# Gate weights scattered into DRAM tables, and two wide passes over the second expert matrix in the first layer

## The chip, the cores and the metric

The kernel runs on one core of one Trainium2 chip. The metric is the device time of one execution in microseconds (us); lower is better. "First layer" is `l = 0` in the code and "second layer" is `l = 1`.

## What is computed

Two layers of a backbone over 512 latent tokens (tiles 0 to 3, 128 tokens each) and 256 context tokens (tiles 4 and 5). The second layer only has to produce the latent tiles. Each layer is token mixing (projection, three kinds of heads, output projection), then the expert retrieval that the change is about:

```python
def peer(h, wq, subkeys, u, v):
    q = (h @ wq).reshape(t, 8, 2, 128)
    s = einsum('thpd,hpnd->thpn', q, subkeys)            # 8 heads, 2 halves, 128 keys each
    s_top, i_top = top_k(s, 16)
    cand = s_top[:, :, 0, :, None] + s_top[:, :, 1, None, :]
    best, pos = top_k(cand, 16)                          # 16 of 128*128 experts per head
    gate = softmax(best)
    a = gelu(einsum('cd,chkd->chk', h, u[expert]))
    return einsum('chk,chkd->cd', gate * a, v[expert])
```

A token thus has 8 x 16 = 128 picks among 16384 experts of 1024 numbers each.

## The kernel before

`peer` (L945) does each layer's retrieval in stages. **Routing and picking** (`routing`, `picks`, `pick`) finds each token's 128 experts and gates. **Two up passes** (`upass`, L994, halves 0 and 1) stream the first expert matrix, 128 slices of 512 KB, and compute every expert's activation for three "dense" tiles (`self.dense`): a slice is split into two half-precision parts (high by ScalarE; low by VectorE or GpSimd, L1003 to L1006), 24 products of 128x384 follow, and Gelu. Two tiles' activations stay in SBUF (tiles `P`), the third's go to DRAM (`spill`). For the tiles that are not dense, `gather` (L912) fetches each pick's row with 128 indirect DMAs on the GpSimd queue (L924), with a dot product on VectorE (L930) each.

**The weight of every expert for every token** must then be laid out as a matrix, expert by token. `Scatter.step` (L1157) builds it: for eight tokens at a time VectorE makes one-hot matrices (L1176, `oi` and `oj`), multiplies one by the gates (L1180, `og`), TensorE multiplies the two (L1185, L1186), and the product is copied or multiplied into `P` (L1190 to L1196).

**Passes over the second expert matrix** (`vpass`, L1032): one for each pair of tiles in `self.groups`, three in the first layer and two in the second. A pass streams 128 slices of 512 KB, splits each (high L1048 on ScalarE; low L1050 on VectorE or L1052 on GpSimd, by `VDVE`), and adds 12 products of 128x512 a slice into four PSUM banks (L1065). `Scatter.at` splits the dense tiles' weights two slices at a time (L1126).

The order of the work is set in two steps. `tick` lets each background generator (`rg` routing, `bg` gathers) advance by a rate for each slice (`RATES`, `RRATE`, L1026, L1029, L1069), and a scheduling layer then fixes each engine's instruction order by priority and data dependency. Each engine runs its list strictly in that order, and so does the SP queue, which issues nearly all plain DMAs. The zeroing of the change goes into `project` (L357), the loop over 12 column chunks with three tile pairs each.

Of the kernel before, what the change touches and what calls it, by code (L numbers as in the profile page):

```python
# [25 lines left out]
US = 64.0  # L26
PS = 16.0
NEG = -1e30
TB = 8
# [3 lines left out]
RATES = {0: (2.0, 1.4, 0.8, 0.9, 0.9, 0.9, 0.0, 0.0), 1: (1.2, 1.3, 0.6, 0.6, 0.0, 0.0)}  # L33
RRATE = (0.9, 0.85)
# [6 lines left out]
WADA = 7  # L41
RL1, RL2 = 1, 0
PF = (1, 1)
UP1 = (24, 24)
SC0 = (12, 12)
PRATE = (0.5, 0.5)
VDVE = ((1, 3), (1, 3), (3,))


class Hybrid:  # L50
    def __init__(self, tc, aps, out):
        self.tc, self.nc, self.i, self.out = tc, tc.nc, aps, out
        self.dbg = {}
        self.bg = []
        self.rg = []
        self.lo_ins = None
# [15 lines left out]
    def consts(self):  # L72
# [12 lines left out]
        nc.vector.tensor_copy(self.iox, io)  # L85
        self.mhalf = c.tile([128, 8], F32, name="mhalf")
# [150 lines left out]
    def layer(self, l, last):  # L237
        with ExitStack() as es:
            self.l, self.last = l, last
            self.rt, self.h2T, self.h2d = {}, {}, {}  # L240
            self.groups = ((2, 3), (0, 1)) if last else ((2, 3), (4, 5), (0, 1))
            self.dense = (2, 3, self.groups[1][1])
            self.picked = [t for g in self.groups for t in g if t not in self.dense]
            tiles = XTILES if last else XTILES + CTILES
            self.mid = {t: self.tc.dram_tile([128, D], F32, name=f"mid{l}_{t}") for t in tiles}
# [20 lines left out]
    def mixers(self, l, last, wes):  # L266
# [11 lines left out]
        with ExitStack() as e:  # L278
            nap = self.pool(e, "nqkv")
            self.naT = nap.tile([128, 4, 2, T], F16, name="naT")  # L280
            self.nav = [nap.tile([128, 2, 2, 256], F16, name=f"nav{p}") for p in range(3)]
            hp = self.pool(e, "hT", 3)
# [14 lines left out]
            self.flush(self.rg)  # L297
            self.flush(self.bg)
# [58 lines left out]
    def project(self, l, last, hp, pool, ps, ap_, att_es, xs):  # L357
# [29 lines left out]
        for ch in range(12):  # L387
# [5 lines left out]
            for pr in (1, 0, 2):  # L393
# [9 lines left out]
                self.tick(self.rg, 1)  # L403
                self.tick(self.bg, RATE_NA if ch < 6 else RATE_DF)
# [280 lines left out]
    def wout(self, l, es, last):  # L685
# [3 lines left out]
        self.h2U = [self.lp.tile([128, KC, 384], F16, name=f"h2U{x}") for x in "hl"]  # L689
# [121 lines left out]
    def picks(self, l, tiles, sv, si, pool):  # L811
        for t in tiles:
            yield from self.pick(l, t, sv[t], si[t], pool)
            if t in self.picked:
                self.bg.append(self.gather(l, t))

# [21 lines left out]
    def pick(self, l, t, sv, si, pool):  # L838
# [25 lines left out]
        st = self.lp.tile([128, 2, 16, 8], F16, name="st", bufs=4 if self.last else 6)  # L864
        sg = self.lp.tile([128, 16, 8], F32, name="sgate", bufs=4 if self.last else 6)
# [27 lines left out]
        nc.vector.tensor_tensor(sg, sg, sm[:, None, :].to_broadcast([128, 16, 8]), op=OP.mult)  # L893
        ix = None
        if t in self.picked:
            ix = self.lp.tile([128, 16, 8], I32, name="ix", bufs=3)
            ef = pool.tile([128, 16, 8], F32, name="ef")
            nc.vector.tensor_scalar(ef, st[:, 0], 128.0, float(l * 16384), op0=OP.mult, op1=OP.add)
            nc.vector.tensor_tensor(ix, ef, st[:, 1], op=OP.add)
            ix = ix.rearrange("p k h -> p (k h)")  # L900
        self.rt[t] = (st.rearrange("p a k h -> p a (k h)"), sg.rearrange("p k h -> p (k h)"), ix)
# [10 lines left out]
    def gather(self, l, t):  # L912
        nc = self.nc
        _, sg, ix = self.rt[t]
# [4 lines left out]
        a = self.lp.tile([128, 128], F32, name="a", bufs=1)  # L919
        rows = []  # L920
        for k in range(128 + AHEAD):
            if k < 128:
# [3 lines left out]
                    in_offset=bass.IndirectOffsetOnAxis(ap=ix[:, k:k + 1], axis=0)))  # L926
                rows.append(r)
            if k >= AHEAD:
                r = rows[k - AHEAD]
                nc.vector.scalar_tensor_tensor(r, r, 1.0, hp, op0=OP.mult, op1=OP.mult,  # L930
                                               accum_out=a[:, k - AHEAD:k - AHEAD + 1])
            if k < 127 + AHEAD:
                yield
        nc.scalar.activation(a, a, AF.Gelu)
        nc.vector.tensor_tensor(sg, a, sg, op=OP.mult)
        self.done.add(t)
        yield
# [3 lines left out]
    def need(self, t):  # L941
        while t not in self.done:
            self.step(self.bg, 1)

    def peer(self, es, l, last, h2s):  # L945
        nc = self.nc
        self.done = set()
        self.hpp = self.pool(es, "hp", 1, space=PSUM)
        self.pw = self.pool(es, "pw", 2, space=PSUM)
        self.gp = self.pool(es, "gat", 3)  # L950
        self.spill = self.tc.dram_tile([128, 128, 128], F32, name=f"spill{l}")
        self.big = [[self.pool(es, "bigA")], []]
        sc = Scatter(self, (2, 3), True)
        sc.P[0] = [self.table(0, 0)]
        rk = ExitStack()
        with ExitStack() as e:
# [4 lines left out]
            groups = ((0, 1), (2, 3)) if last else ((4, 5), (2, 3, 0, 1))  # L961
            self.unscored = len(groups)
            self.rg += [self.routing(l, rt, ps, t, rp) for t in groups]
            self.upass(l, 0, sc, self.pw, "pw", RATES[l][0], RRATE[l])
# [4 lines left out]
        sc.P[1] = [self.table(1, 0)]  # L969

        def more():
# [3 lines left out]
            sc.P[1].append(self.table(1, 1))  # L975

        with ExitStack() as e:
            ps = self.pool(e, "ups", 4, space=PSUM)
            self.upass(l, 1, sc, ps, "pa", RATES[l][1], PRATE[l], more)
        self.accp = self.pool(es, "acc", 1, space=PSUM)  # L980
        for n, tiles in enumerate(self.groups):
            if n == 2:
# [3 lines left out]
            follow = Scatter(self, self.groups[n + 1]) if n + 1 < len(self.groups) else None  # L986
            self.vpass(l, tiles, int(tiles[0] > 3), sc, follow, RATES[l][2 + 2 * n:4 + 2 * n])
            sc = follow
# [5 lines left out]
    def upass(self, l, half, sc, ps, tag, rate, rrate, more=None):  # L994
        nc = self.nc
        ahead = [sc.step(0)] if half else []
        ut = self.i["ut"][l]
        hh, hl = self.h2U
        def load(jj):
# [10 lines left out]
        for jj in range(64):  # L1010
# [6 lines left out]
            for k in range(KC):  # L1017
                self.mm3(pa[:, :384], uh[:, 0, k], uh[:, 1, k], hh[:, k], hl[:, k], k == 0, k == KC - 1)
# [250 lines left out]
```

## Time and profile before

| | |
|---|---|
| median of 3 runs | 4867.58 us (4862.76 to 4879.73) |
| the profiled execution's own time | 4873.35 us |
| its span, first to last instruction | 4871.5 us |
| busy share of the span | PE 84%, PEld 49%, DVE 75%, ACT 45%, POOL 47% |
| mean granted TensorE clock | 0.930 of full speed |

PE is TensorE's matmul, PEld its weight load, DVE is VectorE, ACT is ScalarE, POOL is GpSimd. The span has the following stages. First layer: mixing and output projection to 620.7 us, up passes to 1477.5, passes over the second matrix to 2873.0. Second layer: mixing to 3317.9, up passes to 4073.9, passes over the second matrix to 4853.8. The shares above are means over these stages; what bounds one stage is read from a table by stage.

### The profile page before, as it was taken

Reading aid. Unit: us, or ns where it says so; the run is one execution under the profiler, and the core shown is the slowest. Engines: PE = TensorE matmul, PEld = TensorE weight load, DVE = VectorE, ACT = ScalarE, POOL = GpSimd, SP = SyncE. Lnnn points to the kernel's source line nnn. Section 1 sums busy time; section 2 is a strip of 40 time slices with the busy share of each in tenths; the row PEclk is TensorE's granted clock in tenths of the full one; section 3 lists DMA queues with packets and bytes.
Section 4 is the critical chain, followed back from the end, with each engine's and each line's share of the span. In section 5 each row is a group of like instructions: output and inputs, shape, how many; then the busy total and the mean of one; then the engine's idle time right before and its main releaser. Section 6 shows DMA issues by size and latency. Waiting matters only on the chain. (4 is left out here: it accounts for less than half of the span.)

```text
span 4871.5 us, 79464 instructions
## 1 busy us (share of the span) xinstructions
PE 4102.9 (84%) x30416; PEld 2392.5 (49%) x30416; DVE 3665.2 (75%) x6812; ACT 2188.7 (45%) x3704; POOL 2269.5 (47%) x1557
## 2 busy tenths in 40 slices
PE   4987888977887887787788989878887899997998
PEld 3665465743553333333334447746564554443443
DVE  7677648898779999898899443565767689998663
ACT  4556344444443343333333455655444444454443
POOL 3223223456666666555533432233246665563443
PEclk8997899998999988999999999979999999999999
DMA  5421345657877777887768653124566776555665
GB/s 173 143 86 37 123 141 169 216 190 239 282 260 250 257 252 252 278 275 265 281 212 287 219 184 94 40 85 136 163 200 206 260 272 206 166 183 176 200 205 176
DMA packets 379869, 955.11 MB, mean 196 GB/s; under 512 B 43632, under 2 KB 158800, under 8 KB 379488
## 3 DMA queue, kind: packets, MB, share of 16 engines
q1 hardware_dynamic: 296000, 675.74, 42.5%
q0 software_dynamic: 73888, 268.53, 15.6%
q10 hardware_dynamic: 9600, 5.77, 0.4%
q8 instruction: 238, 3.90, 0.3%
q14 instruction: 143, 1.17, 0.1%
HBM read 920.49 MB, written 29.41 MB: 195 GB/s over the span
## 5 line engine op out<-in xcount | busy, mean ns | idle before, releaser
L1052 POOL TENSOR_TENSOR hl<-s,hl 128x1024 f16<-128x1024 f32 x384 | 880.1, 2296 | 873.8 <-ACT hl L1048 856.6
L1065 PE MATMUL acc<-hl,gst 128*128 128x512 f16 x3456 | 827.1, 388 | 4.9 <-ACT gst L139 4.9
L930 DVE SCALAR_TENSOR_TENSOR r<-r,hp 128x1024 f32<-128x1024 f32 x512 | 618.7, 1212 | 279.6 <-DMA r<-peer_u,ix 278.7
L924 POOL DMA_INDIRECT r<-peer_u,ix x512 | 572.1, 1117 | 428.7 <-DVE r L930 219.3
L1048 ACT ACTIVATE hl<-s 128x1024 f16<-128x1024 f32 x480 | 503.5, 1055 | 581.7 <-PE acc L1065 280.7
L1065 PEld LDWEIGHTS <-gst 128*128 128x128 f16 x4608 | 452.5, 100 | 607.4 <-issue 116.0
L1065 PE MATMUL acc<-hl,P 128*128 128x512 f16 x2304 | 564.6, 389 | 57.6 <-POOL hl L1052 30.2
L1065 PEld LDWEIGHTS <-P 128*128 128x128 f16 x3072 | 296.3, 99 | 428.7 <-issue 95.0
L166 PE MATMUL pw<-h2Uh,hl 128*128 128x384 f16 x1024 | 353.6, 345 | 56.2 <-ACT gst L1022 56.1
L168 PE MATMUL pa<-h2Uh,hl 128*128 128x384 f16 x1024 | 345.8, 338 | 63.6 <-POOL hl L153 36.6
L153 POOL TENSOR_TENSOR hl<-s,hl 128x1024 f16<-128x1024 f32 x136 | 299.0, 2200 | 170.1 <-ACT hl L152 85.1
L1185 PE MATMUL pw<-og,oi 128*128 128x64 f16 x2560 | 203.8, 197 | 205.7 <-DVE og L1180 199.1
L168 PE MATMUL pw<-h2Uh,hl 128*128 128x384 f16 x1024 | 352.5, 344 | 23.5 <-DVE hl L143 17.7
L167 PE MATMUL pw<-h2Ul,hl 128*128 128x384 f16 x1024 | 352.8, 345 | 0.0
L1050 DVE TENSOR_TENSOR h2Ul<-h2Uh,h2Ul 128x1024 f16<-128x1024 f32 x160 | 259.4, 1621 | 123.7 <-ACT h2Ul L1048 123.7
L166 PE MATMUL pa<-h2Uh,hl 128*128 128x384 f16 x1024 | 345.3, 337 | 1.6 <-ACT hl L152 1.6
L167 PE MATMUL pa<-h2Ul,hl 128*128 128x384 f16 x1024 | 345.2, 337 | 0.0
L1176 DVE TENSOR_TENSOR oi<-iox,sT 128x1024 f16<-128x1024 f16 x320 | 321.9, 1006 | 27.5 <-PE pw L1186 26.3
L1065 PE MATMUL acc<-h2Ul,gst 128*128 128x512 f16 x1152 | 289.6, 395 | 53.9 <-DVE h2Ul L1050 53.9
L168 PEld LDWEIGHTS <-hl 128*128 128x128 f16 x2048 | 208.3, 102 | 251.9 <-POOL hl L153 53.8
L151 ACT ACTIVATE s<-s 128x1024 f32<-128x1024 f32 x136 | 143.7, 1057 | 417.7 <-DMA s<-ut 392.7
L1180 DVE TENSOR_TENSOR og<-oj,gT 128x1024 f16<-128x1024 f16 x320 | 322.5, 1008 | 0.6
(297 smaller groups left out, 9587.7 us busy)
## 6 DMA issues: line engine op xcount, KB each, us to landing
s<-peer_v SPq DMA_DIRECT2D x480, 512.0 KB, 4.3
s<-ut SPq DMA_DIRECT2D x256, 512.0 KB, 4.2
h2Uh<-peer_v SPq DMA_DIRECT2D x160, 512.0 KB, 4.0
wq<-peer_wq SPq DMA_DIRECT2D x128, 256.0 KB, 3.8
wst<-w_in SPq DMA_DIRECT2D x96, 256.0 KB, 3.1
r<-w_ada SPq DMA_DIRECT2D x48, 512.0 KB, 5.3
h2T<-w_ada SPq DMA_DIRECT2D x32, 512.0 KB, 3.6
spill<-gst SPq DMA_DIRECT2D x64, 256.0 KB, 4.6
```

What stands on the lines that cost most here:

```text
L153: self.lo_ins = nc.gpsimd.tensor_tensor(lo, w, hi, op=OP.subtract)
L166: nc.tensor.matmul(out, ah, bh, start=start, stop=False)
L167: nc.tensor.matmul(out, ah, bl, start=False, stop=False)
L168: nc.tensor.matmul(out, al, bh, start=False, stop=stop)
L924: self.queue_behind(nc.gpsimd.indirect_dma_start(out=r, out_offset=None, in_=self.i["peer_u"], in_offset=bass.IndirectOffsetOnAxis(ap=ix[: ...
L930: nc.vector.scalar_tensor_tensor(r, r, 1.0, hp, op0=OP.mult, op1=OP.mult, accum_out=a[:, k - AHEAD:k - AHEAD + 1])
L1048: nc.scalar.activation(vh[:, 0], v, AF.Copy)
L1050: nc.vector.tensor_tensor(vh[:, 1], v, vh[:, 0], op=OP.subtract)
L1052: self.lo_ins = nc.gpsimd.tensor_tensor(vh[:, 1], v, vh[:, 0], op=OP.subtract)
L1065: nc.tensor.matmul(acc[s][hf], w, vh[:, x, hf * 512:hf * 512 + 512], start=j == 0 and i == 0, stop=j == 127 and i == 2)
L1176: nc.vector.tensor_tensor(out.rearrange("p t (i x) -> p t i x", x=2), io.rearrange("p (i x) -> p i x", x=2)[:, None].to_broadcast([128, TB ...
L1180: nc.vector.tensor_tensor(og.rearrange("p z t (j x) -> p (z t) j x", x=2), oj.rearrange("p t j -> p (t j)")[:, None].to_broadcast([128, 2, ...
```

## The change

- **Tables.** `Scatter` is gone. Each tile has a `Table` of 8 MB in DRAM, [128 x 128 experts, 128 tokens]. It is filled with zeros during the token mixing by eight DMAs of 1 MB (`clear`, on SP). Then each of a token's 128 picks is written as one 4-byte element at its place by indirect DMAs on the GpSimd queue (`put`): one DMA writes one pick of each of the 128 tokens, 128 DMAs fill a tile, and each group of 16 (a head) waits until the group before it has landed. `vpass` reads the table back two slices at a time (`get`, 128 KB) and multiplies by the activations (`weigh`).
- **Equal picks.** Two heads of a token may pick the same expert; later writes would hide earlier ones. `pick` thus computes for each pick the sum of the gates of all equal picks: 128 VectorE instructions of 128x128 for each tile (`gjk`).
- **Four dense tiles in the first layer** (2, 3, 4, 5; products of 128x512 in the up passes, two tiles spilled), so only tiles 0 and 1 are gathered there (before: 4, 0 and 1). In the second layer 2, 3 and 1 are dense and 0 is gathered, as before.
- **Two passes instead of three** over the second matrix in the first layer, with three tiles each: (2, 3, 4) and (5, 0, 1). The second layer keeps two passes of two tiles.
- **All low splits in `vpass` on VectorE** (`VDVE`).
- Before each pass `need` issues everything that is missing in its tiles' tables. New rates `SRATES` (puts for each slice) and changed `RATES`, `RRATE`.

```diff
-RATES = {0: (2.0, 1.4, 0.8, 0.9, 0.9, 0.9, 0.0, 0.0), 1: (1.2, 1.3, 0.6, 0.6, 0.0, 0.0)}
-RRATE = (0.9, 0.85)
+RATES = {0: (1.6, 1.5, 1.3, 1.3, 0.0, 0.0), 1: (1.2, 1.2, 0.9, 0.9, 0.0, 0.0)}
+SRATES = {0: (2.5, 4.0, 2.5, 4.0, 4.0, 4.0), 1: (2.5, 3.0, 1.5, 2.5, 4.0, 4.0)}
+RRATE = (1.2, 1.0)
...
-VDVE = ((1, 3), (1, 3), (3,))
+VDVE = (0, 1, 2, 3)
...
-            self.groups = ((2, 3), (0, 1)) if last else ((2, 3), (4, 5), (0, 1))
-            self.dense = (2, 3, self.groups[1][1])
+            self.groups = ((2, 3), (1, 0)) if last else ((2, 3, 4), (5, 0, 1))
+            self.dense = (2, 3, 1) if last else (2, 3, 4, 5)
...
+                self.tick(self.zg, 2)
...
+        for k in range(128):
+            jk = pool.tile([128, 128], BF16, name="gjk")
+            nc.vector.scalar_tensor_tensor(jk, e, e[:, k:k + 1], g, op0=OP.is_equal, op1=OP.mult,
+                                           accum_out=o[:, k:k + 1])
...
+    def need(self, tiles):
+        while not all(self.tables[t].full for t in tiles):
+            self.step(self.rg, 1)
             self.step(self.bg, 1)
+            self.step(self.sq, 4)
...
+    def weigh(self, tiles, j, g, u):
...
+        if tiles[0] == self.dense[0]:
+            nc.vector.tensor_tensor(g[:, 0:2], g[:, 0:2], self.col(j // 64, j % 64, 2), op=OP.mult)
+        for s, x in u.items():
+            nc.vector.tensor_tensor(g[:, s], g[:, s], x, op=OP.mult)
+        pr = self.sp.tile([128, 2, len(tiles), 2, 128], F16, name="gst", bufs=GST)
+        self.split(pr[:, 0], pr[:, 1], g)
+        return pr
...
+    def clear(self):
+        o = self.o
+        for c in range(0, 128 * 128, ZC):
+            self.before.append(o.nc.sync.dma_start(self.view()[:, c:c + ZC].rearrange("i (r n) -> i r n", r=4),
+                                                  o.zero[:, None].to_broadcast([128, 4, ZC // 4])))
+            yield
+
+    def put(self, h, to, values, c, step):
...
+        for k in range(16):
+            ins = o.nc.gpsimd.indirect_dma_start(
+                out=self.d, out_offset=bass.IndirectOffsetOnAxis(ap=to[:, k, h:h + 1], axis=0),
+                in_=values[:, c + step * k:c + step * k + 1], in_offset=None)
...
+            self.behind(ins, self.before)
+            o.queue_behind(ins)
+            now.append(ins)
+            if k == 15:
+                self.before = now
...
+    def get(self, dst, j):
+        ins = self.o.nc.sync.dma_start(dst, self.view()[:, j * 128:j * 128 + 256].rearrange("p (j t) -> p j t", t=128))
+        self.behind(ins, self.before)
```

**The order on GpSimd at the end of the first layer's up passes.** `hl` is the low split of a slice of the first matrix, `r<-peer_u` a gather, `table_4` the table of tile 4. Before:

```order
L153 TENSOR_TENSOR hl<-s_16661,hl 128x1024
L924 DMA r<-peer_u,ix 128x1024 x3
L153 TENSOR_TENSOR hl<-s_16760,hl 128x1024
L924 DMA r<-peer_u,ix 128x1024 x2
L153 TENSOR_TENSOR hl<-s_16824,hl 128x1024
L924 DMA r<-peer_u,ix 128x1024 x4
L1052 TENSOR_TENSOR hl<-s_16988,hl 128x1024
```

After:

```order
L1184 DMA table_4_104<-gs,to 2097152x1 x4
L157 TENSOR_TENSOR hl<-s_18101,hl 128x1024
L947 DMA r<-peer_u,ix 128x1024
L1184 DMA table_4_104<-gs,to 2097152x1 x4
L157 TENSOR_TENSOR hl<-s_18144,hl 128x1024
L947 DMA r<-peer_u,ix 128x1024 x2
L1184 DMA table_4_104<-gs,to 2097152x1 x4
L947 DMA r<-peer_u,ix 128x1024
L1184 DMA table_4_104<-gs,to 2097152x1 x4
```

`s_18144` is the last slice of the up passes that GpSimd splits. From there to the last put of table 4 stand 112 puts and 30 gathers; the pass over (2, 3, 4) reads that table.

**The same engine at the end of the second layer's up passes**, where the table of tile 3 is the last that the pass over (2, 3) reads. After:

```order
L157 TENSOR_TENSOR hl<-s_41028,hl 128x1024
L947 DMA r<-peer_u,ix 128x1024 x2
L1184 DMA table_2_26534<-gs,to 2097152x1 x3
L947 DMA r<-peer_u,ix 128x1024
L1184 DMA table_2_26534<-gs,to 2097152x1 x3
L947 DMA r<-peer_u,ix 128x1024 x2
L1184 DMA table_2_26534<-gs,to 2097152x1 x7
L947 DMA r<-peer_u,ix 128x1024
L1184 DMA table_2_26534<-gs,to 2097152x1 x4
L947 DMA r<-peer_u,ix 128x1024
L1184 DMA table_2_26534<-gs,to 2097152x1 x5
L1184 DMA table_3_26535<-gs,to 2097152x1 x16
```

Here `s_41028` is the last slice that GpSimd splits. Behind the last row shown, 4 puts of table 0 and 16 of table 3 (one head) alternate until table 3 is full. From the last split to there stand 178 puts and 7 gathers. Before, no put existed and a pass's own split followed the gathers at once.

## Rows read from the trace of the kernel before

**Rows 1.** Busy time by stage (from:to, length, engines, clock, DMA), nine stages of both layers.

```profile
core 0: us, PE busy (x) PEld busy (x) DVE busy (x) ACT busy (x) POOL busy (x), PEclk, DMA share, GB/s
620.70:1114.30 493.60, 427.06 (x4131) 303.42 (x4129) 380.70 (x1463) 216.16 (x430) 204.67 (x174) 0.94 0.56 180
1114.30:1477.50 363.20, 292.56 (x2071) 172.60 (x2069) 290.05 (x476) 148.36 (x256) 229.40 (x159) 0.92 0.79 266
1477.50:1987.90 510.40, 398.88 (x2584) 188.26 (x2585) 498.38 (x623) 187.64 (x234) 329.59 (x199) 0.91 0.71 250
1987.90:2491.30 503.40, 396.90 (x2582) 186.43 (x2582) 453.36 (x663) 192.03 (x296) 260.84 (x169) 0.93 0.77 268
2491.30:2873.00 381.70, 355.26 (x2002) 164.31 (x2002) 241.33 (x348) 150.42 (x196) 144.06 (x66) 0.99 0.72 239
3317.90:3760.50 442.60, 375.70 (x3266) 254.26 (x3265) 297.27 (x1077) 210.50 (x431) 185.48 (x156) 0.93 0.55 177
3760.50:4073.90 313.40, 276.52 (x2071) 167.07 (x2069) 229.82 (x317) 144.26 (x250) 201.08 (x133) 0.97 0.76 263
4073.90:4493.90 420.00, 377.18 (x2606) 184.86 (x2607) 396.25 (x425) 189.14 (x239) 225.50 (x96) 0.96 0.54 174
4493.90:4853.80 359.90, 349.26 (x1996) 164.00 (x1993) 194.79 (x275) 166.25 (x245) 152.31 (x64) 0.99 0.63 201
```

**Rows 2.** The same view for line 1065 alone (PE, PEld): a gap, and a half pass.

```profile
2474.40:2491.20 16.80, 0.00 (x0) 0.13 (x1) 0.64 0.73 250
2701.40:2873.00 171.60, 167.93 (x768) 75.28 (x768) 0.99 0.64 203
```

**Rows 3.** Costliest groups: line, engine, operation, tile, count | busy us, mean ns | idle before.

```profile
L1180 DVE TENSOR_TENSOR og<-oj,gT 128x1024 f16<-128x1024 f16 x320 | 322.5, 1008 | 0.6
```

**Rows 4.** The same view: VectorE's splits and the multiply into `P`.

```profile
L1050 DVE TENSOR_TENSOR h2Ul<-h2Uh,h2Ul 128x1024 f16<-128x1024 f32 x160 | 259.4, 1621 | 123.7 <-ACT h2Ul L1048 123.7
L141 DVE TENSOR_TENSOR pl<-w,ph 128x768 f16<-128x768 f32 x64 | 60.9, 951 | 39.2 <-ACT ph L139 39.1
L1191 DVE TENSOR_TENSOR P<-pw,P 128x256 f32<-128x256 f32 x128 | 47.7, 413 | 4.7 <-PE pw L1186 4.6
```

**Rows 5.** The gathers on GpSimd: duration ns min/median/max, landing, and the page's group (mean).

```profile
L924 POOL DMA_INDIRECT r<-peer_u,ix x512: 932/962/1957, 804.8 to 4054.7; - x171
...
DMA to landing us min/median/max: 4.1/5.8/8.8
...
L924 POOL DMA_INDIRECT r<-peer_u,ix x512 | 572.1, 1117 | 428.7 <-DVE r L930 219.3
```

**Rows 6.** GpSimd's other work: small plain DMAs that it issues, and low splits.

```profile
L95 POOL DMA_DIRECT2D g1col<-g1col x2: 564/572/580, 2.2 to 3.2; - x2
...
L153 POOL TENSOR_TENSOR hl<-s,hl 128x1024 f16<-128x1024 f32 x136 | 299.0, 2200 | 170.1 <-ACT hl L152 85.1
```

**Rows 7.** Plain DMAs: KB each, median us from issue to landing.

```profile
gsp<-spill SPq DMA_DIRECT2D x128, 128.0 KB, 3.2
```

**Rows 8.** VectorE's dot products over 32 elements (line 624) and 1024 (line 930).

```profile
L624 DVE SCALAR_TENSOR_TENSOR lamj<-lp x6: 179/182/192, 73.7 to 2719.2; 128x32 f32<-128x32 f32 x6
L624 DVE DVE_READ_ACCUMULATOR lamj<-lp x6: 77/80/82, 73.8 to 2719.3; 128x1 f32 x6
...
L930 DVE SCALAR_TENSOR_TENSOR r<-r,hp 128x1024 f32<-128x1024 f32 x512 | 618.7, 1212 | 279.6 <-DMA r<-peer_u,ix 278.7
```

**Rows 9.** Columns of Rows 1: the last 18 slices of both layers' first up pass.

```profile
988.00:1114.30 126.30, 96.24 (x582) 55.44 (x580) 118.33 (x437) 56.16 (x88) 66.51 (x42) 0.89 0.57 186
3640.00:3760.50 120.50, 96.14 (x655) 58.54 (x653) 97.24 (x322) 56.89 (x95) 71.76 (x48) 0.93 0.58 193
```

**Rows 10.** Columns of Rows 1: the projection of the first layer.

```profile
66.60:296.00 229.40, 202.80 (x1879) 154.47 (x1879) 157.38 (x296) 127.22 (x225) 54.12 (x39) 0.95 0.44 136
296.00:413.60 117.60, 103.01 (x979) 82.55 (x977) 76.01 (x145) 69.15 (x155) 26.07 (x21) 0.94 0.14 40
```

More of the change, by code (lines that the diff above doesn't have):

```diff
@@ L688, in wout @@
         ps = self.pool(es, "wps", 2, space=PSUM, side="right")
-        self.h2U = [self.lp.tile([128, KC, 384], F16, name=f"h2U{x}") for x in "hl"]
+        self.h2U = [self.lp.tile([128, KC, 128 * len(self.dense)], F16, name=f"h2U{x}") for x in "hl"]
         a4, b3, xs = {}, {}, {}
@@ L815, in picks @@
                 self.bg.append(self.gather(l, t))
+            else:
+                self.sq += [self.tables[t].put(h, self.rt[t][2], self.rt[t][0], h, 8) for h in range(8)]
     def top16(self, v, ix, src, rest):
@@ L968, in peer @@
         self.big[1].append(self.pool(es, "bigB0", side="right"))
[L969 removed]
+        self.P[1] = [self.table(1, 0)]
         def more():
@@ L974, in more @@
             self.big[1].append(self.pool(es, "bigB1", side="right"))
-            sc.P[1].append(self.table(1, 1))
+            self.P[1].append(self.table(1, 1))
         with ExitStack() as e:
             ps = self.pool(e, "ups", 4, space=PSUM)
-            self.upass(l, 1, sc, ps, "pa", RATES[l][1], PRATE[l], more)
+            self.upass(l, 1, ps, "pa", PRATE[l], more)
+        pws.close()
         self.accp = self.pool(es, "acc", 1, space=PSUM)
         for n, tiles in enumerate(self.groups):
-            if n == 2:
+            self.need(tiles)
+            if n == 1 and not last:
                 r = lambda: self.gp.tile([128, D], F32, name="r")
@@ L992, in table, with col, upass @@
         return self.big[half][c].tile([128, 2, 32 if half else 64, 128], F32, name="P")
-    def upass(self, l, half, sc, ps, tag, rate, rrate, more=None):
+    def col(self, half, jj, n=1):
+        w = 32 if half else 64
+        p = self.P[half][jj // w]
+        return p[:, :, jj % w:jj % w + n] if n > 1 else p[:, :, jj % w]
+    def upass(self, l, half, ps, tag, rrate, more=None):
         nc = self.nc
-        ahead = [sc.step(0)] if half else []
         ut = self.i["ut"][l]
         hh, hl = self.h2U
+        nd = len(self.dense)
+        sb = 4 // (nd - 2)
         def load(jj):
@@ new lines, in upass, with weights @@
+            self.tick(self.bg, RATES[l][half])
+            self.tick(self.sq, SRATES[l][half])
+    def weights(self, tiles, j):
+        nc = self.nc
+        n = len(tiles)
+        g = self.sp.tile([128, n, 2, 128], F32, name="gt", bufs=2)
+        u = {}
+        for s, t in enumerate(tiles):
+            self.tables[t].get(g[:, s], j)
+            if t in self.spill:
+                u[s] = self.sp.tile([128, 2, 128], F32, name="gsp")
+                nc.sync.dma_start(u[s], self.spill[t][:, j:j + 2])
+        return g, u
```

292 lines of the change are left out of this document (116 added, 176 removed).

## The prediction

> **What bounds the kernel now.** I read the busy time by stage first, since the shares of the whole span (PE 84%, DVE 75%, POOL 47%) mix stages with different limits. In the first layer's first two passes over the second matrix DVE is busy 498 of 510 us and 453 of 503; where no weights are built any more, in the third, it is 241 of 382 and PE 355 [rows 1]. What fills DVE there is `Scatter.step`: one of its three large operations alone, `og`, takes 322.5 us [rows 3]. The second layer is the same in small: 420 us for the pass beside the scatter, 360 for the one after it. PE's own speed shows in the second half of the third pass: 768 products of 128x512 in 171.6 us, so .2234 us each, at a granted clock of .99, 2.4 GHz [rows 2].
>
> POOL, which has idle time everywhere, matters for what follows: in the second up passes it is busy 229 of 363 us and 201 of 313 [rows 1], with low splits and gathers.
>
> **The passes.** Removed: all of `Scatter.step`. Added for each pair of slices: a table read, one multiply by the activations, a split. If PE sets the pace, the first layer's two passes take 2 x 2304 x .2234 = 1029 us and one gap of 16.8 [rows 2], 1046 against 1395.5; the second layer's take 2 x 1536 x .2234 = 686 and 17, 703 against 779.9. That is -349 and -77. DVE covers it: for each slice one low split of 1.26 to 1.62 us, half of a 128x768 split of .95, and half of three multiplies of .41 [rows 4], some 2.7 us against PE's 4.0 (18 products). The first pass's early slices also carry 65 gathers and their dot products, for which I add 25: **-400**. Bounds: -426, and -330 if DVE sets the pace in half a pass.
>
> **What POOL must now issue before the first pass.** A put is an indirect DMA of 128 elements; none is in the trace. The nearest row is the gather, also one indirect DMA with 128 indices: .962 us median on POOL, 1.117 in the mean [rows 5]. Below it lies a small plain DMA issued from POOL, .56 [rows 6]. I take .962, because the 128 addresses are there to be worked out in both, and gather means for gathers.
>
> First layer. The first up pass multiplies 128 columns more: 1536 products x a quarter of .2234 = 86 us on PE, 493.6 to 580. In the second, the order shows on POOL 50 low splits, 106 gathers and 249 puts: 50 x 2.2 [rows 6] + 106 x 1.117 + 249 x .962 = 468 us, at 95% busy 493, where PE needs 64 slices x 24 x .2234 = 343 and the pass took 363. Each split stands between puts, so POOL sets the pace. Behind the last split stand 112 puts and 30 gathers until table 4 is full: 108 + 33 = 141 us, in which PE has no work, since `need` stands ahead of the pass. Landing (5.8 [rows 5]), a table read (3.2 [rows 7]) and one multiply and split add 11, and PE's last two slices hide about as much. Sum 580 + 493 + 141 = 1214 against 856.8: **+357**. The remaining tables 5, 0 and 1 (319 puts and 82 gathers, 398 us) lie beside the first pass of 515 us and cost nothing there; at 1.3 us a put that cover would be gone.
>
> Second layer. The first up pass keeps its three dense tiles and its 442.6. The second has 50 splits, 81 gathers and 188 puts: 110 + 90 + 181 = 381, at 95% 401. Behind the last split stand 178 puts and 7 gathers: 171 + 8, and, since a head waits for the head before it to land, 8 x (5.8 - 4 x .962) = 16: 195. Sum 442.6 + 401 + 195 = 1039 against 756.0: **+283**.
>
> That makes 727 puts on the path (361 and 366). The trace shows POOL at work for the whole of a gather. The Trainium skill would have it otherwise: in "DMA: Bandwidth & Descriptors", section "Anatomy of one DMA — SWDGE (gpsimd) path", dispatch is about 50 ns and descriptor generation is small, "You can emit a lot of descriptors before the incremental cost shows up". By it a put would cost POOL an estimated .1 us, the second up passes would keep their length, 45 and 69 us of waits would stand ahead of the passes, and the time would be an estimated 4770. The .962 us of the gathers speaks against that.
>
> **The sums of equal picks on DVE.** 128 instructions of 128x128 a tile with an accumulated output. The nearest rows: .182 us for 32 elements and .08 for reading the accumulator; 1024 elements take 1.21, so 1.04 ns an element [rows 8]. That gives .28 + .08 = .36 us, 46 us a tile, in ten uninterrupted blocks. In the first layer six blocks (276 us) come before the first pass's start. DVE idles 8 us in the last 18 slices of the first up pass and 105 before them [rows 1, 9]; the 86 us of wider products are more room: 199 in all, 77 short. Those are not just late: a gather on POOL waits for the dot product that frees its buffer, and low splits stand behind it. Some of it lies beside the second up pass: I take +60. In the second layer four blocks, 184 us, stand against 145 idle [rows 1, 9]: +25. Together **+85**, between 0 (all beside POOL's queue) and 460 (none hidden).
>
> **Zeros.** 48 MB in the first layer's projection on SP's queue among the `w_in` loads. There the DMAs move 136 GB/s at a share of .44, then 40 [rows 10]; elsewhere 250 at .71 [rows 1], about 350 when full. 48 MB in 229 us are 220 GB/s more: 356, just full. I add 9 us, and 7 for the 32 MB of the second layer: **+15**, between 0 and 60 (a few loads late).
>
> **Sum:** -400 + 357 + 283 + 85 + 15 = +340. The profiled execution took 4873, so 5213; it is 6 above the median of the runs shown, so about 5207: I say **5205**.
>
> **Rivals.**
> 1. *Puts are cheap (the other side).* POOL only starts a put, and the DMA engines do the rest. With p the price of a put, the sum is 340 - 733 x (.962 - p): 765 us for each us on 727 puts at 95% busy, less 32 for the heads' waits. It turns at p = .50 us. At .40 the second layer's second up pass is back at PE's pace (313 instead of 290), and the time is 4867 + 340 - 412 + 23 = **4820**. For: an element of 4 bytes moves almost nothing. Against: even the plain DMAs of [rows 6] take .56, and the gather's time is issue, not transfer. Chance .10. The section of the Trainium skill named above is the rule behind this one.
> 2. *The landing sets the pace.* The program gives each put one of eight completion semaphores, so eight are under way at most; if 4-byte writes land after 12 us instead of 5.8, a put costs 1.5 and the sum grows by 733 x .538 = 394: **5600**. For: 128 separate writes. Against: gathers with 128 rows of 4 KB land in 8.8 at most [rows 5]. Chance .05.
> 3. *The sums of equal picks are not hidden at all*: 460 instead of 85, **5580**. For: 94% busy DVE in the last 18 slices [rows 9]. Against: the last three blocks of the first layer stand behind the splits that PE waits for. Chance .05.
> 4. Everything nearly cancels, with puts about .5: 4868. Chance .03.
>
> **How the numbers follow.** The forecast, POOL's issue of puts as the bound, has .77 and a range of its own from 5000 to 5450 (puts from .75 to 1.12, the sums of picks from 0 to 250). Rival 1, 2 and 3 lie mostly outside; the range reaches down to half of the way to rival 1: 4850 to 5450, which leaves out .20. Within .3% (15 us) counts as no change; slower by more than that are the forecast and rivals 2 and 3, .87; the same .03; faster .10.
>
> **What would show it.** Right: puts of about .96 us on POOL; POOL busy nearly throughout the second up passes, which take some 490 and 400 us; PE idle for some 140 us ahead of the first layer's first pass, waiting for a table, and 195 in the second; half passes without a gather at .223 us a product; blocks of 46 us on DVE; the projection longer by some 10 us. Wrong: a put below half a microsecond, up passes at their old length, or passes that run slower than PE, with DVE or the table reads as what ended its waits.

## The result and the profile after

The changed kernel takes **5755.84 us** (median of 4 runs, 5751.85 to 5765.23) against 4871.85 for the kernel before beside it: ratio 1.1818, interval 1.1791 to 1.1845. It is slower, as forecast, but by 884 us and not by 340; the time lies above the predicted range. Two of the versions below, half the indices and the memset on VectorE, also had executions 2% and 4% longer than the profiled one (5938, and three between 5890 and 5913), and only the profiled one is compared.

Busy time by stage of the changed kernel, columns as in [rows 1]: the projection, then for the first layer the two up passes, the wait ahead of the first pass, and the passes in three pieces; for the second layer the two up passes, the wait, and the passes.

```profile
66.90:409.80 342.90, 303.37 (x2827) 236.26 (x2826) 228.05 (x425) 193.62 (x373) 80.48 (x58) 0.95 0.73 248
621.00:1244.00 623.00, 504.96 (x4131) 299.88 (x4130) 508.50 (x2307) 223.73 (x432) 272.04 (x238) 0.92 0.45 140
1244.00:1857.70 613.70, 404.32 (x1537) 160.51 (x1534) 335.41 (x1038) 156.48 (x255) 479.10 (x413) 0.83 0.51 164
1857.70:2034.20 176.50, 0.00 (x0) 0.00 (x0) 38.76 (x63) 3.96 (x8) 133.25 (x137) 0.51 0.35 103
2034.20:2376.80 342.60, 266.76 (x1100) 113.61 (x1101) 199.28 (x280) 88.16 (x97) 264.10 (x242) 0.91 0.73 235
2376.80:2484.00 107.20, 0.03 (x1) 0.00 (x0) 2.29 (x4) 0.12 (x1) 77.87 (x82) 0.52 0.09 24
2484.00:3300.00 816.00, 769.94 (x3508) 344.73 (x3507) 453.18 (x564) 276.37 (x304) 97.94 (x81) 0.98 0.80 265
3752.00:4290.00 538.00, 385.01 (x3268) 254.33 (x3266) 388.01 (x1725) 208.57 (x427) 255.38 (x227) 0.88 0.44 139
4290.00:4765.60 475.60, 307.95 (x1535) 162.70 (x1534) 219.08 (x561) 147.27 (x251) 385.64 (x323) 0.84 0.53 172
4765.60:5001.40 235.80, 0.07 (x2) 0.04 (x2) 13.29 (x20) 3.61 (x7) 179.65 (x183) 0.51 0.10 26
5001.40:5733.00 731.60, 676.41 (x3071) 301.18 (x3072) 449.69 (x518) 335.28 (x383) 69.66 (x67) 0.99 0.77 242
```

Against the sum, stage by stage (us; the sums of equal picks put where the prediction had them):

| stage | before | predicted | after | after less predicted |
|---|---|---|---|---|
| first layer, first up pass | 494 | 640 | 623 | -17 |
| second up pass | 363 | 493 | 614 | +121 |
| wait ahead of the first pass | none | 141 | 176 | +35 |
| passes over the second matrix | 1396 | 1071 | 1266 | +195 |
| second layer, first up pass | 443 | 468 | 538 | +70 |
| second up pass | 313 | 401 | 476 | +75 |
| wait | none | 195 | 236 | +41 |
| passes | 780 | 703 | 732 | +29 |

The eight differences sum to 549, which is also 5756 - 5207: the stages not listed, the 15 us for the zeros and the step from the profiled execution to the median cancel to within 2 us. Three readings of the trace explain most of it.

**The period of a put.** GpSimd's timeline in the second layer's wait (start, length, operation, idle before it):

```profile
4879.67 0.96 POOL L1184 DMA_INDIRECT table<-gs,to  x1 [0.30 <-issue]
4880.94 0.96 POOL L1184 DMA_INDIRECT table<-gs,to  x1 [0.30 <-issue]
```

A put is busy for .97 us, as taken, but the next starts 1.27 us after it: .30 lie between them, in which the engine waits for nothing that shows. GpSimd is thus full at a busy share of .76 (180 of 236 us in the wait), where the prediction had .95 in the up passes and 1 in the waits. In that wait 183 instructions, all of them indirect DMAs, take 236 us, 1.29 each; a gather in a row of them also starts 1.29 us after the one before (median of 130 pairs). The kernel before shows the same for two gathers in a row:

```profile
932.04 0.96 POOL L924 DMA_INDIRECT r<-peer_u,ix  x1 [0.16 <-issue]
933.30 0.94 POOL L924 DMA_INDIRECT r<-peer_u,ix  x1 [0.30 <-DVE rest L821]
```

1.26 from start to start. The profile puts this .30 down to VectorE, but it is the same .30 as above, where nothing shows. So the period could have been read before the change.

**A hole of 107 us in the first layer's first pass**, in which no engine but GpSimd works. The waits of SP's queue (the one that issues the plain DMAs) between 2300 and 2500 us (total, times, longest), its timeline, and the memset on GpSimd:

```profile
SPq L1175 <- POOL zero L289: 112.1, 1, 112.1
```

```profile
2363.02 0.32 SPq L1074 DMA_DIRECT2D gsp<-spill  x1
2475.53 0.37 SPq L1175 DMA_DIRECT2D table<-zero  x1
```

```profile
2474.96 0.54 POOL L289 MEMSET zero<- 128x512 f32 x1
```

The second layer has its own tile of zeros, filled by a memset on GpSimd (L289). The scheduling layer placed the first zeroing DMA of that layer early on SP, since nothing but the tile held it back; the memset stands on GpSimd behind puts of the pass and runs at 2474.96. SP waits for it, and every table read and slice load of the pass stands behind SP.

**Dot products whose gathers stand among puts.** In the same pass from 2036 to 2370 us, VectorE's and TensorE's longest waits:

```profile
DVE r L953 <- DMA r<-peer_u,ix: 102.5, 48, 6.7
```

```profile
PE acc L1121 <- DVE hl L1107: 63.1, 18, 8.0
PE acc L1121 <- DVE h2Ul L1107: 12.7, 6, 4.3
```

VectorE has time to spare there (199 of 343 us busy), but its list is strict: a dot product waits for its gather, and behind it stands the low split that TensorE needs.

The zeros cost the first layer's projection nothing: it takes 343 us where it took 347 [rows 10], with the DMAs at .73 instead of .44 and .14. The 32 MB of the second layer are not written in its own projection: the last zeroing DMA starts at 2759 us, still inside the first layer's passes.

### The profile page after: what moved, and what is told of

Same layout as the page of the kernel before. It is cut to its first block, busy times and chain, and to the rows that moved or that the text cites. A ratio compares the mean times of both kernels' runs of the same rounds, so it can differ in the third digit from the quotient of the medians.

```text
span 5750.0 us, 72469 instructions
## 1 busy us (share of the span) xinstructions
PE 4162.7 (72%) x25266; PEld 2239.7 (39%) x25266; DVE 3297.0 (57%) x8245; ACT 2023.1 (35%) x3287; POOL 2545.8 (44%) x2328
## 3 DMA queue, kind: packets, MB, share of 16 engines
q8 instruction: 198, 3.24, 0.2%
## 5 line engine op out<-in xcount | busy, mean ns | idle before, releaser
L1121 PE MATMUL acc<-hl,gst 128*128 128x512 f16 x5760 | 1308.6, 386 | 656.6 <-ACT gst L143 412.3
L1121 PEld LDWEIGHTS <-gst 128*128 128x128 f16 x7680 | 759.6, 99 | 1650.3 <-ACT gst L143 413.2
L1184 POOL DMA_INDIRECT table<-gs,to x896 | 907.8, 1013 | 325.5 <-issue 251.7
L172 PE MATMUL pa<-h2Uh,hl 128*128 128x512 f16 (+1 forms) x1024 | 410.0, 401 | 353.8 <-POOL hl L157 325.3
L1107 DVE TENSOR_TENSOR hl<-s,hl 128x1024 f16<-128x1024 f32 x384 | 468.5, 1220 | 79.5 <-ACT hl L1105 78.5
L920 DVE SCALAR_TENSOR_TENSOR gjk<-ef,sgate 128x128 bf16<-128x128 f32 x1280 | 495.0, 454 | 0.0
L1184 POOL DMA_INDIRECT table<-a,to x384 | 408.7, 1064 | 156.5 <-issue 143.0
L172 PE MATMUL pw<-h2Uh,hl 128*128 128x512 f16 (+1 forms) x1024 | 378.5, 370 | 115.9 <-DVE hl L147 81.8
L170 PE MATMUL pa<-h2Uh,hl 128*128 128x512 f16 (+1 forms) x1024 | 407.9, 398 | 23.2 <-ACT hl L156 20.7
L170 PE MATMUL pw<-h2Uh,hl 128*128 128x512 f16 (+1 forms) x1024 | 380.3, 371 | 34.0 <-ACT gst L1054 33.7
L171 PE MATMUL pa<-h2Ul,hl 128*128 128x512 f16 (+1 forms) x1024 | 403.9, 394 | 0.0
L171 PE MATMUL pw<-h2Ul,hl 128*128 128x512 f16 (+1 forms) x1024 | 378.5, 370 | 0.0
```

The lines of the kernel that those rows point to most:

```text
L170: nc.tensor.matmul(out, ah, bh, start=start, stop=False)
L171: nc.tensor.matmul(out, ah, bl, start=False, stop=False)
L172: nc.tensor.matmul(out, al, bh, start=False, stop=stop)
L920: nc.vector.scalar_tensor_tensor(jk, e, e[:, k:k + 1], g, op0=OP.is_equal, op1=OP.mult, accum_out=o[:, k:k + 1])
L1107: nc.vector.tensor_tensor(vh[:, 1], v, vh[:, 0], op=OP.subtract)
L1121: nc.tensor.matmul(acc[s][hf], pr[:, w, s, j % 2], vh[:, x, hf * 512:hf * 512 + 512], start=j == 0 and i == 0, stop=j == 127 and i == 2)
```

## The experiments

**What the puts cost in all.** Only the last pick of each head is put:

```diff
         for k in range(16):
+            if k < 15:
+                yield
+                continue
             ins = o.nc.gpsimd.indirect_dma_start(
```

> Only one of a head's 16 picks is put (the others get weight zero). Theory (the issue of puts holds the second up passes, the waits ahead of the first passes and the zeroing): the second up passes fall to TensorE's pace, 614 to about 363 and 476 to about 313, the waits from 176 to 45 and from 236 to 45, and the gap of 107 us goes: 5756 - 251 - 163 - 131 - 191 - 107 = about 4910. Rival (VectorE's sums of equal picks and the table reads hold these stages): above 5300.

Measured: **4919.92** (ratio to before 1.0114, 1.0072 to 1.0156), ten above the number expected. Its second up passes and the wait between them, by stage:

```profile
1221.80:1696.10 474.30, 364.72 (x1537) 155.31 (x1534) 330.02 (x1122) 154.25 (x253) 240.25 (x179) 0.87 0.63 213
1696.10:1746.80 50.70, 0.04 (x2) 0.01 (x1) 29.40 (x48) 3.77 (x7) 29.18 (x28) 0.54 0.80 268
3793.30:4143.40 350.10, 272.12 (x1536) 153.75 (x1534) 223.33 (x673) 144.31 (x250) 206.51 (x147) 0.90 0.68 234
```

The puts are worth 836 of the 884 us. That the theory's total came out is luck in part: the first layer's second up pass stayed at 474 instead of 363, because sums of equal picks are left over from the first and run beside it (without them it takes 340, below), while its first up pass and its passes came out 21 and 60 us shorter than the theory had them, and the second layer's first up pass 42.

**What one put costs.** Puts into a tensor that nothing reads are added (`d2` exists for the tables of tiles 2 and 3 of the second layer):

```diff
             now.append(ins)
+            if self.d2 is not None:
+                ins = o.nc.gpsimd.indirect_dma_start(
+                    out=self.d2, out_offset=bass.IndirectOffsetOnAxis(ap=to[:, k, h:h + 1], axis=0),
+                    in_=values[:, c + step * k:c + step * k + 1], in_offset=None)
...
+                now.append(ins)
```

> In the second layer every put of the tables of tiles 2 and 3 is issued a second time, into a DRAM tensor that nothing reads: 256 more puts ahead of the first pass. The second up pass and the wait behind it take 712 us in the changed kernel. Theory (each put costs the path the 1.27 us from one start to the next): 712 + 325 = about 1040. By the prediction's price (.962 at 95% busy, 1.013): 712 + 259 = 970. If the puts were not on the path: 712.

Measured: **6058.46**. The second up pass and the wait of the second layer:

```profile
4282.00:4889.20 607.20, 336.56 (x1538) 168.06 (x1535) 216.44 (x569) 148.58 (x252) 485.62 (x427) 0.79 0.41 135
4889.20:5315.70 426.50, 0.04 (x1) 0.04 (x2) 12.45 (x20) 3.48 (x7) 324.40 (x336) 0.51 0.06 14
```

607 + 427 = 1034, so 322 us for 256 puts, 1.26 each: the period, and not 1.013.

**What the price hangs on.** Half the indices:

```diff
-ap=to[:, k, h:h + 1]   in_=values[:, ...]
+ap=to[0:64, k, h:h + 1]   in_=values[0:64, ...]
```

> Each put has 64 indices instead of 128 (tokens 64 to 127 of a tile get no weights). Back-to-back puts of the changed kernel start every 1.27 us, .97 of it busy. If that is a price of the instruction (theory), the period stays near 1.27 and the time within 40 us of 5756. If it is paid for each index (rival 1), the period falls to about .8 and the time by 727 x .47 = 340, to about 5415. If the landing of eight puts under way sets the period (rival 2), it falls with the landing, and GpSimd waits for DMAs, not for nothing that shows.

Measured: 5818.37, not shorter. All puts of gates, and two starts in the second layer's wait:

```profile
L1184 POOL DMA_INDIRECT table<-gs,to x896: 891/897/1935, 1110.5 to 4968.0; - x180
```

```profile
4947.69 0.90 POOL L1184 DMA_INDIRECT table<-gs,to  x1 [0.30 <-issue]
4948.90 0.89 POOL L1184 DMA_INDIRECT table<-gs,to  x1 [0.30 <-issue]
```

64 indices fewer take .07 us off: the period is 1.20 to 1.21 instead of 1.27, so the price is nearly all the instruction's. (The medians over all puts in a row are 1.20 and 1.28; some stretches of this run, such as 4953 to 4968 us, have 1.40.) Rivals 1 and 2 of that expectation fall: the idle time between two puts stays at .30 and is put down to nothing that shows, not to a DMA. By stage the run did gain ahead of the passes: second up passes and waits take 770 and 698 us instead of 790 and 712, 34 of the 727 x .07 = 50 us that the period would give. It lost more in the passes, which take 1295 and 824 instead of 1266 and 732. There TensorE waits 170 and 83 us for nothing that shows, which it does not in the changed kernel's first profile (last section).

**The memset.** `self.nc.gpsimd.memset(self.zero, 0.0)` becomes `self.nc.vector.memset(self.zero, 0.0)`.

> In the changed kernel the second layer's first zeroing DMA stands on SP's queue inside the first layer's first pass, and waits 112 us for a memset on GpSimd that stands behind some ninety puts; every load behind it on SP waits too, and TensorE is idle for 107 us. Here the memset is on VectorE instead. Theory: the gap goes, 5756 - 107 = about 5650. Rival: GpSimd's puts would have held the pass anyway, within 20 us of 5756.

Measured: 5667.71 in the profiled execution; the end-to-end gain alone rests on that one and would be unclear. In its trace the hole is gone and the two passes take 1184 us instead of 1266. Two versions below that keep this edit and are otherwise close to the changed kernel came to 5641 and 5650. The hole's cause is shown for the executions that have it. 82 of its 107 us came back; TensorE has 66 us of waits for nothing that shows in these passes, which the changed kernel's first profile had not (last section). Not every execution has the hole: when the changed kernel was measured again, SP did not wait for the memset; TensorE crawled through that stretch instead, and the two passes took 1307 us.

**The sums of equal picks.** The 128 instructions a tile are replaced by one copy of the gates:

```diff
-            nc.vector.scalar_tensor_tensor(jk, e, e[:, k:k + 1], g, op0=OP.is_equal, op1=OP.mult,
-                                           accum_out=o[:, k:k + 1])
+            if k == 0:
+                nc.vector.tensor_tensor(o, g, g, op=OP.max)
```

> The gates are copied instead of summed over equal picks (a token whose heads pick one expert twice gets one gate of the two). Ten blocks of 128 instructions, some 58 us each by the changed kernel's trace, leave VectorE. Theory: the first up passes lose what exceeded TensorE's own work, 623 to about 580 and 538 to about 443, and the second ones little, as GpSimd holds them: about 5756 - 140 = 5615. Rival: GpSimd's queue is the bound throughout, within 30 us of 5756.

Measured: **5567.56** (1.1445, 1.1398 to 1.1493), 188 less. The four up passes:

```profile
619.80:1190.90 571.10, 506.85 (x4131) 301.56 (x4129) 407.45 (x1599) 228.49 (x437) 286.55 (x250) 0.94 0.51 166
1190.90:1746.00 555.10, 399.60 (x1537) 159.18 (x1534) 138.00 (x212) 149.74 (x250) 454.12 (x399) 0.87 0.51 168
3652.50:4132.00 479.50, 387.69 (x3268) 255.64 (x3265) 299.65 (x1092) 211.81 (x433) 263.92 (x236) 0.92 0.50 164
4131.80:4588.60 456.80, 299.57 (x1538) 159.37 (x1535) 111.98 (x169) 141.17 (x245) 375.29 (x316) 0.87 0.51 170
```

-52, -59, -58 and -19. The second up passes gain too, which the theory did not expect. In the first layer's, GpSimd's longest waits of the changed kernel for VectorE are these:

```profile
POOL r L947 <- DVE r L953: 22.6, 29, 3.3
POOL r L947 <- DVE bv L834: 12.9, 1, 12.9
```

A gather waits for the dot product that frees its buffer, or for a pick, while VectorE works on sums; without the sums both waits are gone (.3 and none). Puts wait for the gates that the sums produce only in the first up passes, 21 and 19 us.

**What is left without either.** Both edits together.

> One put of 16 and no sums of equal picks (weights of the other 15 picks are zero, equal picks are not summed): what is left of the change is the two wide passes, the wider products and the table reads. Theory: from the 4920 with one put of 16, the first up passes go to about 580 and 443 and the second ones to about 400 and 330, so 4750, some 115 below the kernel before. Rival (the passes or VectorE still hold what the sums held): 4900 or more.

Measured: **4629.32**, ratio .9514 (.9458 to .9571), 121 us better than expected. The up passes of the first layer and, 54 us later, its passes:

```profile
618.50:1171.40 552.90, 494.12 (x4130) 299.23 (x4129) 420.12 (x1600) 229.97 (x438) 216.05 (x183) 0.96 0.53 172
1171.40:1511.70 340.30, 334.03 (x1537) 150.26 (x1535) 136.62 (x214) 148.93 (x247) 217.14 (x163) 0.99 0.79 273
1565.30:2659.30 1094.00, 1015.83 (x4608) 452.88 (x4608) 661.28 (x864) 365.58 (x402) 118.38 (x94) 0.98 0.82 276
```

The second up pass runs at TensorE's pace (340; 343 was the number for it), and the passes in 1094. With next to no weights (one put of 16 is left) the change would be worth 236 us; the weights cost 1127. Puts alone are worth 836 and sums alone 188; together 103 more, since each hides part of the other (the first layer's second up pass: 474 without puts, 555 without sums, 340 without either).

**Moving work off GpSimd, or elsewhere on it.** Four versions tried to use the period of 1.27 us.

The low splits of the up passes go to VectorE (`UPOOL = ((), ())`, `UP0 = (64, 64)`, `UP1 = (0, 0)`):

> All low splits of the up passes are on VectorE, none on GpSimd; nothing else changes. Theory (GpSimd's queue sets the length of the second up passes and of the waits behind them): 50 splits of 2.2 us leave that path in each layer, so 5756 - 2 x 110 = about 5535. Rival (VectorE, with the sums of equal picks, is as full as GpSimd): the splits cost there what they save here, within 60 us of 5756.

Measured: **6010.99**, neither. TensorE's longest waits between 1200 and 1700 us, the end of the first up pass and the start of the second:

```profile
PE pw L172 <- DVE hl L147: 191.5, 6, 93.6
PE pa L172 <- DVE hl L147: 110.2, 2, 96.3
```

The splits of the last 18 slices now stand on VectorE between the blocks of sums, and these blocks became longer. VectorE's timeline in a block of sums of the changed kernel, and in one of this version (the steps without their accumulator reads):

```profile
820.07 0.34 DVE L920 SCALAR_TENSOR_TENSOR gjk<-ef,sgate 128x128 bf16<-128x128 f32 x1
820.34 0.07 DVE L920 DVE_READ_ACCUMULATOR gjk<-ef,sgate 128x1 f32 x1
820.34 0.34 DVE L920 SCALAR_TENSOR_TENSOR gjk<-ef,sgate 128x128 bf16<-128x128 f32 x1
```

```profile
1246.05 0.35 DVE L920 SCALAR_TENSOR_TENSOR gjk<-ef,sgate 128x128 bf16<-128x128 f32 x1 [2.44 <-remote]
1248.15 0.35 DVE L920 SCALAR_TENSOR_TENSOR gjk<-ef,sgate 128x128 bf16<-128x128 f32 x1 [1.74 <-remote]
1250.96 0.35 DVE L920 SCALAR_TENSOR_TENSOR gjk<-ef,sgate 128x128 bf16<-128x128 f32 x1 [2.45 <-issue]
```

A step that follows the one before at once starts .27 us after it (the read of the accumulator lies inside the next step's .34); here one starts every 2.1 or 2.8 us, although each is still busy for .35. So the run says nothing on the question it was made for.

Three passes of two tiles in the first layer, three dense tiles, memset on VectorE (in short; the lines are drawn together):

```diff
-else ((2, 3, 4), (5, 0, 1))    dense (2, 3, 4, 5)    routing ((0, 1), (2, 3, 4, 5))
+else ((2, 3), (4, 5), (0, 1))  dense (2, 3, 5)       routing ((4, 5), (2, 3, 0, 1))
-RATES[0] (1.6, 1.5, 1.3, 1.3, 0, 0)            SRATES[0] (2.5, 4, 2.5, 4, 4, 4)
+RATES[0] (1.2, 1.0, 1.2, 1.2, 1.2, 1.2, 0, 0)  SRATES[0] (2.5, 4, 2.5, 2.5, 2.5, 2.5, 4, 4)
```

> First layer back to three passes of two tiles and three dense tiles, with the tables kept, and the memset on VectorE. PE multiplies in the passes what it multiplied in two wide ones (3 x 343 against 2 x 515), the first up pass loses its 86 us of wider products, and 74 indirect DMAs fewer stand ahead of the first pass (133 gathers and 416 puts, by the order). Theory (the wide passes gave nothing that the tables had not given): 5668 - 60 - 100 - 60 = about 5440. Rival (a pass more costs a pass more of loads and splits): above 5750.

Measured: **5870.84** (1.2053, 1.1898 to 1.2209): the theory falls. In the profiled execution (5914) up passes and wait do take 1285 us instead of 1413, but the three passes take 1501. The first two thirds of that time:

```profile
1903.20:2403.00 499.80, 324.40 (x1166) 123.56 (x1167) 303.22 (x425) 129.46 (x151) 360.97 (x319) 0.84 0.75 243
2403.00:2903.00 500.00, 332.38 (x1283) 131.63 (x1281) 336.39 (x481) 153.32 (x184) 308.01 (x262) 0.86 0.87 297
```

TensorE is busy for two thirds of that time; GpSimd issues a DMA every 1.6 to 1.9 us there, and the DMA engines move 243 and 297 GB/s. A third pass streams 64 MB once more, and TensorE waits 168 us in the passes for weights (beside the 133 ahead of them), where in the changed kernel it had no such wait within the passes. Beside these puts and gathers two wide passes are thus worth more than three narrow ones; which of the loads, the gathers and the puts holds the narrow ones is not shown.

The same with the splits on VectorE, tiles 2 and 3 routed first, and most gathers in the passes (`RATES` (0.6, 0.9, 1, 1, 1, 1, 0, 0) and (0.3, 0.3, 0.8, 0.8, 0, 0), with `SRATES` to match):

> As the run with pairs, and besides: up-pass splits on VectorE, tiles 2 and 3 routed first, so that only 256 puts and 6 gathers stand ahead of the first layer's first pass, and nearly all gathers moved into the passes; in the second layer likewise 256 puts and 13 gathers. Theory (GpSimd issues about one indirect DMA in 1.28 us all the time, and what counts is how many stand ahead of each pass): the first layer's second up pass and wait fall from 790 us to about 450, the second layer's from 712 to about 420, and the passes' queues (425 and 473 DMAs ahead of the second and third) just hold them: about 5000, between 4850 and 5200. Rival (VectorE becomes the bound, with sums, dots and all splits): above 5300.

Measured: **5895.41** (1.2099, 1.207 to 1.2129): the rival's time, for its reason in part (at the end of the first up pass TensorE waits 75 us for a pick and 49 for a split on VectorE, and once 99 for nothing that shows). The wait ahead of the first layer's first pass is gone, and nothing was gained by it: the up passes alone take 1336 us, where up passes and wait had taken 1413, and the three passes 1504. In the second layer the second up pass takes 579 us where it and the wait had taken 712 (420 were expected), but the first up pass grows from 538 to 619 and the passes from 732 to 763.

The second layer's gathers moved behind the start of its first pass (`RATES[1] = (0, 0, 2, 2, 0, 0)`), memset on VectorE:

> Memset on VectorE, and in the second layer no gather before the first pass but what the wait there issues (28, by the order, instead of all 128; 60 puts of that tile fewer too). Theory: 160 indirect DMAs leave the path ahead of the first pass, some 200 us of the second layer's two up passes and wait; in the first pass VectorE then stands in its order behind dot products whose gathers wait among puts, which costs about 60: 140 less than with the memset alone (5668), about 5530. Rival: the first pass grows by what the up passes lose.

Measured: **5641.12** (1.1594, 1.1535 to 1.1652), 27 below the one execution with the memset alone. The second layer's second up pass, wait and passes:

```profile
4161.20:4535.30 374.10, 275.83 (x1538) 152.67 (x1535) 87.52 (x286) 138.75 (x239) 290.07 (x237) 0.93 0.32 101
4535.30:4723.10 187.80, 0.00 (x0) 0.00 (x0) 40.35 (x63) 3.40 (x7) 140.88 (x145) 0.51 0.31 96
4723.10:5620.30 897.20, 730.79 (x3072) 310.19 (x3072) 563.81 (x726) 336.38 (x390) 255.40 (x226) 0.92 0.78 256
```

Second up pass and wait went from 712 to 562, and the passes from 732 to 897: the rival. GpSimd's DMAs only changed place.

In the first layer's first pass the gathers go first (`RATES[0][2:4]` = 4, 4; `SRATES[0][2]` = 0), memset on VectorE:

> Memset on VectorE, and in the first layer's first pass the 65 gathers come first, four a slice, and the puts behind them. In the changed kernel VectorE waits 102 us there for gathers, in front of splits that TensorE waits for (76 us). Theory (a gather is late because puts stand between gathers): most of that goes, 50 less than with the memset alone. Rival (the DMA engines are full with gathers, tables and slices): no change.

Measured: **5650.49**, 17 below the memset alone. VectorE's waits for gathers fall to 59 us, but the puts now end late, and 66 us of waiting stand between the two passes (2615 to 2681). Moved again, not removed.

The changed kernel itself, beside the others:

> The changed kernel itself, beside the others on this chip: 5756 within 0.5% by every theory.

Measured: 5802.07 (1.1913, 1.1885 to 1.1941), .8% longer than the first time. All comparisons of some 20 to 50 us must be read with that in mind, those of the two versions above with the memset alone among them. Stage lengths of the up passes and waits agree within 3 us between these two runs; the first layer's passes differ by 41.

No version that computes the same beats the kernel before; the one that would, 4629, has hardly any weights.

## Why the prediction was wrong

**Right.** The direction and its mechanism: puts on GpSimd set the length of the second up passes and the waits, and TensorE idles ahead of each first pass. The passes: -400 was predicted, and without puts and sums they take 1094 and 720 against 1396 and 780, which is -361. The up pass with wider products (86 predicted) went from 494 to 553 there. The zeros, +15 with 0 as the lower bound, cost nothing as bandwidth in the projection.

**The step that failed** is the price of a put, "I take .962", "at 95% busy". The nearest row was the right one; its busy time was not the price. From start to start two indirect DMAs in a row take 1.27 us, and doubling the puts cost 1.26 each. The sum had 1.013 for the 437 puts of the second up passes and .962 for the 290 of the waits (its slope of 765 us for each us, in rival 1, takes 95% for both, a slip): at 1.27 they cost 112 and 89 us more. The 224 gathers among them, at 1.29 from start to start instead of 1.18 (187 of them) and 1.117 (37), cost about 28 more. Some 230 of the 272 us by which the second up passes and waits exceed the sum are thus the price. Rivals 1 and 2 are out: the put is not cheap, and its landing does not set the pace (with half the indices the period changed by .07 us).

**Cover that was named but not priced.** The tables that "lie beside the first pass of 515 us and cost nothing there" had their break at 1.3 us a put, and the period is 1.27: GpSimd was nearly full for the first pass. (The prediction counts 82 gathers there in one place and 65 in another; the trace has 63.) The gathers there got 25 us; VectorE waited 102 for them and TensorE 76 for VectorE.

**Not foreseen at all:** SP's wait for a memset on GpSimd, 107 us of idle TensorE in the execution that was profiled. The prediction counted the zeroing DMAs as bandwidth in the projection and did not ask what their source tile waits for, nor where the scheduler had put the second layer's first one; it stands in SP's order ahead of loads of the first layer's first pass.

**The sums of equal picks**, "+85", are worth 188. The size of a step was not the miss: back to back one starts every .27 us where .36 was estimated, and with some slower ones VectorE is busy with all of them for 495 us where the ten blocks were 460. What was too large is the part taken as hidden. The prediction names the path (a gather waits for the dot product that frees its buffer) and takes 60 us for the first layer without working them out; the waits above show it, and the puts' waits of 21 and 19 us beside it. They do not account for all of the 103 us between.

These misses, some 230, 107, 51 (76 less 25) and 103 us, make some 490 of the 549; they overlap, so this is no exact sum.

The Trainium skill's sentence that I set against the gathers' row ("DMA: Bandwidth & Descriptors", "Anatomy of one DMA — SWDGE (gpsimd) path", many descriptors before the cost shows) agrees with these runs in one half: 64 indices more cost .07 us. The cost of the instruction, .97 busy and 1.27 from start to start, is not in its 50 ns of dispatch.

## What to carry to other kernels

Price an instruction that will stand in a queue by the distance between two starts in a row, not by its busy time: an engine can be full at a busy share of .76. The distance can be longer than the busy time (a put, 1.27 against .97) or shorter (a step of the sums, .27 against .34 and .08). When work goes to a queue, count everything that must pass that queue in the stretch, the pass behind it included, and ask of every new DMA what its source waits for and what stands behind it on its own queue. Where the queue was full, reordering it moved a wait from one stage to the next (three versions); only fewer instructions shortened it.

## What the runs showed of the hardware

Several versions (half the indices, splits on VectorE, the reordered one), and the changed kernel when it was measured again, show an engine that crawls without waiting for anything: in the version with splits on VectorE a step of the sums starts every 2.1 or 2.8 us, and with half the indices TensorE's products do the same in the second layer's first pass:

```profile
5031.47 0.58 PE L1121 MATMUL acc<-hl,gst 128*128 128x512 f16 x1 [1.52 <-issue]
5034.26 0.59 PE L1121 MATMUL acc<-hl,gst 128*128 128x512 f16 x1 [2.21 <-issue]
```

The changed kernel measured again has it in the first layer's first pass, where the first profile has the hole (from:to, length, columns as in [rows 1]):

```profile
2380.00:2480.00 100.00, 21.05 (x36) 3.71 (x36) 4.27 (x5) 2.85 (x3) 71.98 (x74) 0.50 0.07 16
```

GpSimd issues puts back to back in most of these stretches, but the two do not end together: here the last put ahead of a pause starts at 2483.83 and TensorE is back at full pace at 2490; with half the indices the last put starts at 5064.59 and TensorE crawls on to 5090.

The DMA queues do not show the cause. With half the indices, from 4990 to 5090 us, no packet of TensorE's instruction queue (q8) is recorded among these:

```profile
q1 hardware_dynamic: 1013, 2.11, 6.3%
q0 software_dynamic: 1832, 0.02, 1.1%
q14 instruction: 1, 0.01, 0.0%
```

and in the changed kernel, which at the same place has the same puts and runs at full pace (5010 to 5100 us), there are three:

```profile
q1 hardware_dynamic: 9913, 22.74, 81.7%
q8 instruction: 3, 0.05, 0.2%
```

That does not show that instructions arrive late. Over the whole run q8 brings 3.24 MB in 198 packets, and TensorE executes 50532 products and weight loads: 64 bytes for each (as in the kernel before, 3.90 MB for 60832), so some 255 instructions a packet; in the 100 us of the crawl TensorE ran 71, which need a third of one, and in the 90 us at full pace 834. The loads of that stretch are few as well (21 against 254 GB/s), and they too may follow from the crawl, since a slice's buffers come free only as TensorE uses them. So whether late instructions or something else holds the engine is open, and so is why one run has it and another with the same rate of puts has not; no run here was made to settle it. With half the indices TensorE's waits for nothing that shows sum to 253 us in the passes, more than the run gained ahead of them. That the crawl is also why splits on VectorE, between blocks of 256 short instructions, lost 255 us is likely but not shown.
